# Softmax reciprocals sent through DRAM as rows instead of single numbers, and a later division

## The chip, the cores and the metric

One core of a Trainium2 chip runs the whole kernel. The metric is the device time of one execution in microseconds. The kernel before was timed three times: 1243.27, 1243.87 and 1244.43 us, a median of 1243.87. Every reading below is from one profiled execution, which took 1240.66 us with a span of 1238.9 us from its first to its last instruction.

## What is computed

The reference is two decoder layers on a sequence of 512 positions and a width of 1024. The change concerns the first layer's attention alone: 8 heads "A" (sparse attention: for each query only the 128 best keys of an index score count, with a bias by distance) and 8 heads "B" (forgetting attention: cumulated gates as bias), all causal. Cut to what matters:

```python
la = einsum('bthr,btkr->bhtk', ql, c_sel) + bias            # heads A
pa = softmax(where(valid, la, -inf));  oa = einsum('bhtk,btkr->bthr', pa, c_sel)
lb = einsum('bthd,bshd->bhts', qb, k_b) + fq - cum_f_keys   # heads B
pb = softmax(where(causal, lb, -inf)); ob = einsum('bhts,bshd->bthd', pb, v_b)
x  = layer_norm(ALPHA * x + concat([oa, ob]) @ w_o)
# then a convolutional FFN, and a second layer with gated mixers and another FFN
```

The softmax's division by the sum over keys may be done after the product with the values. The kernel does that.

## The kernel before

Every matrix product keeps float32 accuracy by three products: each operand is split into a rounded part and a rest ("hi" and "lo"), and `mm3` (lines 156 to 158) multiplies hi by hi, hi by lo and lo by hi. ScalarE makes hi by a cast, VectorE or GpSimd makes lo by a subtraction (`cut2`, lines 194 and 195, for results in PSUM).

Weights come as a stream of 192 units of 128 x 1024 numbers (`Stream`). SP issues the loads (line 60) into three raw buffers; `_split` casts on ScalarE (line 76) and subtracts on GpSimd (line 78) for the units of `POOL_CUT`, on VectorE (line 80) for the others. Unit 0 holds the index keys and gates, 1 to 4 the index queries, 5 the latent keys, 6 to 9 the values of heads B, 10 to 17 queries and keys of heads B in pairs, 18 to 22 those of heads A, 23 to 30 the output projection.

The 16 heads run in a software pipeline over `for h in range(18)`. The string `SEQ` gives the order within a turn: L the logits of head h (TensorE), B the bias of head h + 1 (GpSimd), T the transposes of head h - 1's probabilities (TensorE, then `cut2`), S the softmax of head h (VectorE adds the bias and takes the minimum of the negated logits, line 585; ScalarE takes exponentials and their sums, line 587), V the values of head h - 2 (TensorE). A digit takes so many steps of `fill`: projections of later heads' queries and keys, eight steps of three products a unit. `step` interleaves rounds of the choice of the best 128 keys on VectorE. The order within each engine's queue is settled at compile time by a list scheduler that starts from this order and may draw instructions forward; at run time each engine's queue works strictly in its order.

The product V yields the head's output transposed: 64 features on partitions, 512 positions along the row. The division needs the reciprocals of the sums along the row too, the same on all partitions, but `soft2` has them as 128 positions x 4 blocks. So they go through DRAM: `rd_d[h]` is written from `rd` with swapped axes (line 593), and `values` reads it back, broadcast to 64 partitions (line 626). Both are on SP's queue, as are the loads of weights. After every second head `values` multiplies (line 634), casts (635) and subtracts (636), the first and last of these on GpSimd for all pairs but the last.

Buffers: `tmp` holds eight tiles of 128 x 512 (the rows of gate sums `fks`, the choice's work tile, `t` and `rb` of `values`), `tri` is one group of three PSUM banks for the transposes, `psh` five banks for logits, values and fills, `dp` three tiles of probabilities `d`, `ptp` two of transposed ones. After the loop these PSUM pools are closed and eight banks opened for the output projection `out_ln`, whose first four units multiply heads B.

Of the kernel before, what the change touches and what calls it, by code (L numbers as in the profile page):

```python
# [9 lines left out]
F32 = mybir.dt.float32  # L10
FR = mybir.dt.float32r
AF = mybir.ActivationFunctionType
ALU = mybir.AluOpType
# [4 lines left out]
D = 1024  # L18
NCH = 4
# [6 lines left out]
EPS = 1e-5  # L26
BIG = 1e30
TAIL = 4
SEQ = "L2BT2SV2"
POOL_CUT = range(5, 23)  # L30
S1, S2, S3, S4 = 4, 3, 1, 2


def _f(ap):
    return ap.bitcast(F32)
# [59 lines left out]
def _body(ctx, tc, A):  # L95
    nc = tc.nc
# [6 lines left out]
    sm = E(tc.tile_pool(name="sm", bufs=4))  # L103
    dr = E(tc.tile_pool(name="dr", bufs=1, space=bass.MemoryType.DRAM))
# [4 lines left out]
    def bank():  # L109
        return ps[0].tile([128, 512], F32, name="bank")  # L110

    def temp():
        return tmp.tile([128, 512], F32, name="temp")

    def quad(dt=FR):
        return quads.tile([128, 4, 512], dt, name="quad")

    ws = Stream(nc, A["ws"], rawp, wp, 2)
    ws.on_pool = POOL_CUT
    base = [0]  # L120

    def unit():
        i = base[0]
        base[0] += 1
        return ws.get(i)
# [17 lines left out]
    ident = cst.tile([128, 128], F32)  # L143
# [10 lines left out]
    def mm3(out, a, b, first, last):  # L154

        nc.tensor.matmul(out, a[0], b[0], start=first, stop=False)  # L156
        nc.tensor.matmul(out, a[0], b[1], start=False, stop=False)  # L157
        return nc.tensor.matmul(out, a[1], b[0], start=False, stop=last)  # L158
# [12 lines left out]
    def proj(w, xt):  # L171
        p = bank()
        half(w, xt, p, 0, S)
        return p
# [8 lines left out]
    def proj_t(us, xt, n):  # L183

        p = bank()
        for k in range(8):
            o = (k % 2) * 512
            last_mm[0] = mm3(p, xk(xt, k, n * 128, n * 128 + 128), wk(us[k // 2], o, o + 512), k == 0, k == 7)
        return p

    def cut2(hi, lo, p, scale=1.0):

        if scale == 1.0:
            nc.scalar.copy(hi, p)
            dve[0] = nc.vector.tensor_tensor(out=lo, in0=p, in1=_f(hi), op=ALU.subtract)  # L195
        else:
            nc.scalar.mul(hi, p, scale)
            dve[0] = nc.vector.scalar_tensor_tensor(out=lo, in0=p, scalar=scale, in1=_f(hi),
                                           op0=ALU.mult, op1=ALU.subtract)
# [138 lines left out]
    with ExitStack() as m0:  # L338
# [9 lines left out]
        p = proj(w, xq)  # L348
# [7 lines left out]
        e = temp()  # L356
# [16 lines left out]
        for m in range(4):  # L373
            p = bank()
            half(unit(), xq, p, 128, S)
            for s, (a, b) in enumerate(((slice(0, 64), slice(64, 128)), (slice(64, 128), slice(0, 64)))):
                nc.scalar.mul(qi[s][a, m, lt], p[a, lt], float(HD ** -0.5))
                nc.vector.scalar_tensor_tensor(out=qi[s][b, m, lt], in0=p[a, lt], scalar=float(HD ** -0.5),
                                               in1=_f(qi[s][a, m, lt]), op0=ALU.mult, op1=ALU.subtract)

        p = bank()
# [9 lines left out]
        p = proj(unit(), xq)  # L391
# [5 lines left out]
        rb = mc.tile([32, NH], F32)  # L397
        nc.gpsimd.dma_start(rb, A["rel_bias"])
        p = bank()
        nc.tensor.matmul(p[:NH, :384], rb, oh[:32, :384], start=True, stop=True)  # L400
        t = temp()
# [3 lines left out]
        p = bank()  # L405
# [51 lines left out]
        def step(n=1):  # L457
            for _ in range(n):
                next(bg, None)
# [4 lines left out]
        for n in range(NCH):  # L464
            p = proj_t(us, xq, n)
# [83 lines left out]
        oq = []  # L549

        def dslice(d, j):
            return d[:, OFF[j]:OFF[j] + 128 * (j + 1)]

        st_ = {}
# [3 lines left out]
        def bias(h):  # L558
            if h < 16:
                biases[h] = (bias_b if h < 8 else bias_a)(h % 8)  # L560

        def logits(h):

            q = made[h // 2]
            d = biases.pop(h)
            r = slice(64 * (h % 2), 64 * (h % 2) + 64)
            b01, b2, b3 = bank(), bank(), bank()
            lg = [b01[:, :128], b01[:, 128:384], b2[:, :384], b3]
            for j in range(NCH):
                n = 128 * (j + 1)  # L570
                c = slice(j * 128, j * 128 + 128)
                mm3(lg[j], (q[r, 0, c], q[r, 1, c]), (q[r, 2, :n], q[r, 3, :n]), True, True)
            st_[h] = (d, lg)

        rd_d = dr.tile([16, NCH, 128], F32, name="rd_d")

        def soft(h):

            d, lg = st_[h]
            mn = sm.tile([128, 4], F32, name="mn")  # L580
            den = sm.tile([128, 4], F32, name="den")
            rd = sm.tile([128, 4], F32, name="rd")
            for j in range(NCH):
                dj = dslice(d, j)
                dve[0] = nc.vector.tensor_tensor_reduce(out=dj, in0=lg[j], in1=dj, scale=1.0, scalar=3e38,
                                               op0=ALU.add, op1=ALU.min, accum_out=mn[:, j:j + 1])
                nc.scalar.activation(dj, dj, AF.Exp, bias=mn[:, j:j + 1], scale=-1.0, accum_out=den[:, j:j + 1])
            st_[h] = (d, den, rd)

        def soft2(h):  # L590
            d, den, rd = st_[h]
            nc.vector.reciprocal(rd, den)
            nc.sync.dma_start(rd_d[h].rearrange("a b -> b a"), rd)

        PO = [0, 512, 896, 1152]

        def turn(h):
            d = st_[h][0]
            p = tri.tile([128, 1536], F32, name="tri")
            for i in range(NCH):  # L600
                for j in range(i, NCH):
                    o = PO[i] + (j - i) * 128
                    nc.tensor.transpose(p[:, o:o + 128], d[:, OFF[j] + i * 128:OFF[j] + i * 128 + 128], ident)
            pt = ptp.tile([128, 2, 1280], FR, name="pt")
            cut2(pt[:, 0], pt[:, 1], p[:, :1280])
            st_[h] = pt

        oq = []
        ot = {}

        def values(h):
            pt = st_.pop(h)
            if h % 4 == 0:
                oq.append(quad())
            i = h // 2
            o = (oq[-1][:, i % 2], oq[-1][:, 2 + i % 2])
            v = vB if h < 8 else vA
            b0 = 64 * (h % 2)
            r = slice(b0, b0 + 64)
            p = bank()  # L620
            m = b0 + 64
            hv = h % 8
            if h % 2 == 0:
                ot[i] = (temp(), temp())
            t, rb = ot[i]
            nc.sync.dma_start(rb[r], rd_d[h].rearrange("a b -> (a b)").partition_broadcast(64))
            for k in range(NCH):
                f = slice(64 * hv - b0, 64 * hv + 64)
                c = slice(PO[k], PO[k] + 512 - 128 * k)
                mm3(p[:m, k * 128:], (v[0][:, k, f], v[1][:, k, f]), (pt[:, 0, c], pt[:, 1, c]), k == 0, k == NCH - 1)  # L630
            nc.scalar.copy(t[r], p[r])  # L631
            if h % 2 == 1:
                eng = nc.gpsimd if h < 15 else nc.vector
                eng.tensor_tensor(out=t, in0=t, in1=rb, op=ALU.mult)
                nc.scalar.copy(o[0], t)
                eng.tensor_tensor(out=o[1], in0=t, in1=_f(o[0]), op=ALU.subtract)

        def work():
            for i in range(2, 4):
# [9 lines left out]
        def fill(n):  # L649
            for _ in range(n):  # L650
                next(todo, None)
# [2 lines left out]
        ps[0] = psum.enter_context(tc.tile_pool(name="psh", bufs=5, space=PSUM))  # L654
        tri = psum.enter_context(tc.tile_pool(name="tri", bufs=1, space=PSUM))
        bias(0)
        for h in range(18):
            for c in SEQ:
                if c == "L" and h < 16:
                    while h // 2 not in finished and next(todo, "end") != "end":  # L660
                        pass
                    logits(h)
                elif c == "B":
                    bias(h + 1)
                elif c == "S" and h < 16:
                    soft(h)
                    step(S3)
                    soft2(h)
                    step(S4)
                elif c == "T" and 1 <= h <= 16:  # L670
                    turn(h - 1)
                elif c == "V" and h >= 2:
                    values(h - 2)
                elif c.isdigit():
                    fill(int(c))
# [16 lines left out]
    with ExitStack() as m1:  # L692
# [17 lines left out]
        for n in range(NCH):  # L710
            p = proj_t(us, xt, n)
            if n < 2:
                late[n](last_mm[0])
            t = vp.tile([128, 8, HD], F32, name="vt")
# [12 lines left out]
            t = t.rearrange("p a b -> p (a b)")  # L727
# [5 lines left out]
        for n in range(NCH):  # L733
            p = proj_t(us, xt, n)
# [3 lines left out]
        for gp in range(4):  # L738
            p = bank()
# [5 lines left out]
            for j in range(2):  # L745
# [3 lines left out]
                    out=uq[:, :, f], in0=p[:, j * 256:j * 256 + 256].rearrange("p (a b) -> p a b", a=4),  # L749
                    scalar=sb[:, gi:gi + 1], in1=uq[:, :, f], op0=ALU.add, op1=ALU.mult)  # L750
        oq = [quad() for _ in range(4)]
        for ft in range(4):
            p = bank()
# [3 lines left out]
        for i in range(4):  # L757
# [5 lines left out]
            t = temp()  # L763
            nc.scalar.mul(t, y, ocw[:, i, 2:3])
            for dlt in (1, 2):
                nc.vector.scalar_tensor_tensor(out=t[:, dlt:], in0=y[:, :S - dlt], scalar=ocw[:, i, 2 - dlt:3 - dlt],
                                               in1=t[:, dlt:], op0=ALU.mult, op1=ALU.add)
            pb = proj(unit(), xt)
            nc.vector.tensor_tensor(out=t, in0=pb, in1=t, op=ALU.mult)
            q = oq[2 + i // 2]  # L770
# [95 lines left out]
```

## Time and profile before

| | |
|---|---|
| median of three runs | 1243.87 us |
| profiled execution | 1240.66 us |
| its span | 1238.9 us |
| TensorE busy | 1168.8 us, 94% of the span |
| VectorE busy | 685.8 us, 55% |
| ScalarE busy | 463.8 us, 37% |
| GpSimd busy | 201.9 us, 16% |
| mean granted TensorE clock | 0.971 |

Busy time on TensorE counts pipelined products whole, so neighbours overlap; the distance from start to start tells the rate. A slice is a fortieth of the span, 31 us; its digit is the busy share in tenths. A row of the waits reads: engine, line that waited, what released it, total us, times, longest. A row of the timeline reads: start, duration, engine, line, operation, output and inputs, count, and in brackets the idle time before it with its releaser. SPq is SP's queue of DMA issues; their duration is the issue alone, and landing is told apart.

### The profile page before, as it was taken

How to read it: one execution, taken by the hardware profiler on the slowest of the kernel's cores; microseconds unless marked ns; L12 is line 12 of the kernel's file. 1: busy time of each engine (PE TensorE's matmuls, PEld its weight loads, DVE VectorE, ACT ScalarE, POOL GpSimd, SP SyncE). 2: the span in 40 equal slices, each digit the busy share in tenths (PEclk: the TensorE clock that was granted, in tenths of full speed). 3: DMA queues.
4: the chain of work that ended last, by engine and by line, in shares of the span. 5: the costliest groups of instructions: out<-in, count | busy, mean ns of one | idle time of the engine just before them, and what ended most of it. 6: DMA issues, size and time to landing. Idle time of an engine off the chain costs nothing. (4 is left out here: it accounts for less than half of the span.)

```text
span 1238.9 us, 14423 instructions
## 1 busy us (share of the span) xinstructions
PE 1168.8 (94%) x5512; PEld 972.1 (78%) x5512; DVE 685.8 (55%) x1120; ACT 463.8 (37%) x693; POOL 201.9 (16%) x254
## 2 busy tenths in 40 slices
PE   7999998535999999999999999999999999999997
PEld 7787886434898888888888788888988888888886
DVE  6779854312656656656223885447565665662236
ACT  7525654422234443443222414233344344342121
POOL 3555653310300000000000420013000000000003
PEclk9999998767999999999999999999999999999999
DMA  6612511225213233234334313354123322344321
GB/s 227 216 66 69 94 14 30 60 61 179 93 60 98 90 102 102 88 106 147 121 118 170 111 52 121 126 184 166 60 94 102 102 88 99 102 140 149 102 85 69
DMA packets 49413, 132.03 MB, mean 107 GB/s; under 512 B 13800, under 2 KB 13808, under 8 KB 49344
## 3 DMA queue, kind: packets, MB, share of 16 engines
q1 hardware_dynamic: 44288, 115.39, 29.5%
q0 software_dynamic: 5056, 15.71, 4.1%
q8 instruction: 43, 0.70, 0.3%
q14 instruction: 26, 0.21, 0.1%
HBM read 122.63 MB, written 10.02 MB: 107 GB/s over the span
## 5 line engine op out<-in xcount | busy, mean ns | idle before, releaser
L156 PE MATMUL bank<-quad,whi 128*128 128x512 f32 (+2 forms) x932 | 356.5, 383 | 6.3 <-ACT quad L137 6.3
L157 PE MATMUL bank<-quad,whi 128*128 128x512 f32 (+2 forms) x932 | 355.6, 382 | 0.5 <-DVE quad L138 0.5
L158 PE MATMUL bank<-quad,wlo 128*128 128x512 f32 (+2 forms) x932 | 355.1, 381 | 0.0
L80 DVE TENSOR_TENSOR wlo<-raw,whi 128x1024 fp32r<-128x1024 f32 x150 | 183.6, 1224 | 291.3 <-ACT whi L76 290.6
L76 ACT CAST whi<-raw 128x1024 fp32r<-128x1024 f32 x161 | 169.6, 1053 | 262.0 <-PE bank L158 115.3
L156 PEld LDWEIGHTS bank<-quad,whi 128*128 128x128 f32 x932 | 176.1, 189 | 41.0 <-ACT quad L137 6.3
L157 PEld LDWEIGHTS bank<-quad,whi 128*128 128x128 f32 x932 | 176.5, 189 | 33.6 <-DVE quad L138 1.1
L158 PEld LDWEIGHTS bank<-quad,wlo 128*128 128x128 f32 x932 | 176.4, 189 | 32.9
L156 PE MATMUL bank<-whi,quad 128*128 128x512 f32 x388 | 151.5, 392 | 17.8 <-ACT temp L631 17.8
L157 PE MATMUL bank<-wlo,quad 128*128 128x512 f32 x388 | 151.6, 391 | 0.0
L158 PE MATMUL bank<-whi,quad 128*128 128x512 f32 x388 | 151.3, 390 | 0.0
L213 POOL DMA_DIRECT2D temp<-x x24 | 13.1, 548 | 567.9 <-ACT quadx L324 424.6
L156 PE MATMUL bank<-quad 128*128 128x512 f32 (+5 forms) x280 | 100.4, 362 | 2.3 <-DVE quad L195 1.4
L157 PE MATMUL bank<-quad 128*128 128x512 f32 (+5 forms) x280 | 98.7, 354 | 0.8 <-DVE quad L80 0.8
L156 PEld LDWEIGHTS bank<-whi,quad 128*128 128x128 f32 x388 | 73.2, 189 | 33.2 <-ACT temp L631 18.0
L158 PE MATMUL bank<-quad 128*128 128x512 f32 (+5 forms) x280 | 98.5, 353 | 0.0
L158 PEld LDWEIGHTS bank<-whi,quad 128*128 128x128 f32 x388 | 73.3, 189 | 15.3
L157 PEld LDWEIGHTS bank<-wlo,quad 128*128 128x128 f32 x388 | 73.3, 189 | 15.2
L293 DVE SCALAR_TENSOR_TENSOR temp<-bank,fcw,temp 128x511 f32<-128x511 f32 x88 | 65.4, 743 | 9.1 <-ACT temp L292 9.1
L80 DVE TENSOR_TENSOR quad<-raw,quad 128x1024 fp32r<-128x1024 f32 x24 | 31.2, 1306 | 68.3 <-ACT quad L76 67.9
L295 DVE SCALAR_TENSOR_TENSOR temp<-bank,fcw,temp 128x510 f32<-128x510 f32 x88 | 65.9, 748 | 3.0
L156 PEld LDWEIGHTS bank<-quad 128*128 128x128 f32 (+1 forms) x280 | 52.6, 189 | 14.6 <-issue 3.6
(148 smaller groups left out, 1293.0 us busy)
## 6 DMA issues: line engine op xcount, KB each, us to landing
raw<-in_ws_dram SPq DMA_DIRECT2D x192, 512.0 KB, 3.5
x<-temp SPq DMA_DIRECT2D x24, 256.0 KB, 2.0
temp<-x POOLq DMA_DIRECT2D x24, 256.0 KB, 3.2
temp<-in_xT_dram SPq DMA_DIRECT2D x8, 256.0 KB, 5.5
temp<-fk_d SPq DMA_DIRECT2D x8, 256.0 KB, 4.4
temp<-rd_d SPq DMA_DIRECT2D x16, 128.0 KB, 4.4
temp<-in_x_dram POOLq DMA_DIRECT2D x8, 256.0 KB, 8.3
quad<-in_ln_g_dram POOLq DMA_DIRECT2D x4, 512.0 KB, 6.0
```

Source lines behind the costliest of these rows:

```text
L76: nc.scalar.copy(hi, t)
L80: dve[0] = nc.vector.tensor_tensor(out=lo, in0=t, in1=_f(hi), op=ALU.subtract)
L156: nc.tensor.matmul(out, a[0], b[0], start=first, stop=False)
L157: nc.tensor.matmul(out, a[0], b[1], start=False, stop=False)
L158: return nc.tensor.matmul(out, a[1], b[0], start=False, stop=last)
L213: nc.gpsimd.dma_start(t, src[n * 128:n * 128 + 128, hf * 512:hf * 512 + 512])
L293: nc.vector.scalar_tensor_tensor(out=t[:, 1:], in0=p[:, :S - 1], scalar=cw[:, j, 1:2], in1=t[:, 1:], op0=ALU.mult, op1=ALU.add)
L295: nc.vector.scalar_tensor_tensor(out=t[:, 2:], in0=p[:, :S - 2], scalar=cw[:, j, 0:1], in1=t[:, 2:], op0=ALU.mult, op1=ALU.add)
```

## The change

The reciprocals of two heads (a pair) are gathered in one tile of 128 x 8. With the odd head's transposes TensorE turns them into 8 rows of 128; ScalarE copies the rows to SBUF and its own queue writes them to `rd_d`, whose layout is now 8 x 8 x 128. The read-back of both halves follows behind the pair's values, on SP. Multiplication, cast and subtraction move out of `values` into `divide`, which stands a head later, before the next V (the letter D), and the loop has two turns more for it. Pairs 0 to 3 divide on GpSimd, 4 to 7 on VectorE. `POOL_CUT` starts at unit 10 instead of 5: 13 units instead of 18 have their second part on GpSimd.

```diff
-SEQ = "L2BT2SV2"
-POOL_CUT = range(5, 23)
+SEQ = "L2BT2SDV2"
+POOL_CUT = range(10, 23)
...
-        rd_d = dr.tile([16, NCH, 128], F32, name="rd_d")
+        rd_d = dr.tile([8, 2 * NCH, 128], F32, name="rd_d")
+        rds = {}
...
         def soft2(h):
-            d, den, rd = st_[h]
-            nc.vector.reciprocal(rd, den)
-            nc.sync.dma_start(rd_d[h].rearrange("a b -> b a"), rd)
+            d, den = st_[h]
+            if h % 2 == 0:
+                rds[h // 2] = sm.tile([128, 8], F32, name="rd")
+            o = 4 * (h % 2)
+            nc.vector.reciprocal(rds[h // 2][:, o:o + 4], den)
...
+            if h % 2 == 1:
+                nc.tensor.transpose(p[:8, 1280:1408], rds.pop(h // 2), ident)
+                row = temp()[:8, :128]
+                nc.scalar.copy(row, p[:8, 1280:1408])
+                nc.scalar.dma_start(rd_d[h // 2], row)
             pt = ptp.tile([128, 2, 1280], FR, name="pt")
             cut2(pt[:, 0], pt[:, 1], p[:, :1280])
...
-                ot[i] = (temp(), temp())
-            t, rb = ot[i]
-            nc.sync.dma_start(rb[r], rd_d[h].rearrange("a b -> (a b)").partition_broadcast(64))
+                ot[i] = [temp()]
+            t = ot[i][0]
...
             if h % 2 == 1:
-                eng = nc.gpsimd if h < 15 else nc.vector
-                eng.tensor_tensor(out=t, in0=t, in1=rb, op=ALU.mult)
-                nc.scalar.copy(o[0], t)
-                eng.tensor_tensor(out=o[1], in0=t, in1=_f(o[0]), op=ALU.subtract)
+                rb = temp()
+                for e in range(2):
+                    nc.sync.dma_start(rb[64 * e:64 * e + 64], rd_d[i, 4 * e:4 * e + 4].rearrange(
+                        "a b -> (a b)").partition_broadcast(64))
+                ot[i].append(rb)
+
+        def divide(i):
+            t, rb = ot.pop(i)
+            q = oq[i // 2]
+            o = (q[:, i % 2], q[:, 2 + i % 2])
+            eng = nc.gpsimd if i < 4 else nc.vector
+            eng.tensor_tensor(out=t, in0=t, in1=rb, op=ALU.mult)
+            nc.scalar.copy(o[0], t)
+            eng.tensor_tensor(out=o[1], in0=t, in1=_f(o[0]), op=ALU.subtract)
...
-        for h in range(18):
+        for h in range(20):
...
+                elif c == "D" and h >= 4 and h % 2 == 0:
+                    divide(h // 2 - 2)
...
-                elif c == "V" and h >= 2:
+                elif c == "V" and 2 <= h <= 17:
                     values(h - 2)
```

More of the change, by code (lines that the diff above doesn't have):

```diff
@@ L581, in soft @@
             den = sm.tile([128, 4], F32, name="den")
-            rd = sm.tile([128, 4], F32, name="rd")
             for j in range(NCH):
@@ L587, in soft @@
                 nc.scalar.activation(dj, dj, AF.Exp, bias=mn[:, j:j + 1], scale=-1.0, accum_out=den[:, j:j + 1])
-            st_[h] = (d, den, rd)
+            st_[h] = (d, den)
         def soft2(h):
-            d, den, rd = st_[h]
-            nc.vector.reciprocal(rd, den)
-            nc.sync.dma_start(rd_d[h].rearrange("a b -> b a"), rd)
+            d, den = st_[h]
[3 more added lines that the diff above has]
+            nc.vector.reciprocal(rds[h // 2][:, o:o + 4], den)
         PO = [0, 512, 896, 1152]
@@ L615, in values @@
             i = h // 2
-            o = (oq[-1][:, i % 2], oq[-1][:, 2 + i % 2])
             v = vB if h < 8 else vA
```

## The prediction

> **What bounds the kernel now.** I read the 40 slices first, then the same stretch in windows, then who waited for whom in it, then SP's own waits and the transfers, then single instructions.
>
> ```profile
> PE   7999998535999999999999999999999999999997
> ```
> ```profile
> core 0: us, PE busy (x) PEld busy (x) DVE busy (x) ACT busy (x) POOL busy (x), PEclk, DMA share, GB/s
> 97.00:186.00 89.00, 89.00 (x479) 71.76 (x479) 69.77 (x183) 53.77 (x119) 51.37 (x78) 0.98 0.30 55
> 186.00:293.00 107.00, 56.73 (x285) 45.26 (x283) 30.27 (x70) 36.76 (x78) 27.03 (x38) 0.73 0.25 56
> ```
>
> TensorE has one hole, the seventh to the tenth slice. In the windows it lies between 186 and 293 us: 56.73 of 107 us busy, at a granted clock of 0.73, while no other engine is busy for even 37 us. Before it TensorE is full. So a wait holds this stage, not an engine's work. Next stand the waits of that window, SP's longest wait over the head loop, the transfers (KB each, us from issue to landing), the spread of the 16 reads' landings, and the ends of the chain on SP.
>
> ```profile
> POOL temp L634 <- DMA temp<-rd_d: 41.4, 3, 20.0
> ACT quad L635 <- POOL temp L634: 39.7, 4, 13.0
> ...
> PE bank L156 <- ACT pt L194: 26.0, 3, 14.4
> ...
> ACT quad L76 <- DMA raw<-in_ws_dram: 20.9, 1, 20.9
> ...
> PE bank L156 <- ACT temp L631: 17.8, 1, 17.8
> ```
> ```profile
> SPq L626 <- DMA rd_d<-rd: 156.8, 16, 11.7
> ```
> ```profile
> rd_d<-rd SPq DMA_DIRECT2D x16, 2.0 KB, 11.0
> ...
> tb_d<-temp POOLq DMA_DIRECT2D x1, 12.0 KB, 3.7
> ```
> ```profile
> DMA to landing us min/median/max: 2.7/4.4/12.5
> ```
> ```profile
> 101.73 0.38 SPq L593 DMA_DIRECT2D rd_d<-rd  x1
> ...
> 284.81 0.45 SPq L626 DMA_DIRECT2D temp<-rd_d  x1
> 285.32 33.94 SPq L60 DMA_DIRECT2D raw<-in_ws_dram  x10
> ```
>
> Read from the bottom up: SP issues write, read, write, read for 16 heads, one after the other. Each read waits until its own write of 2 KB has landed, 11.0 us after issue. From the first write to the last read are 183.1 us, 11.4 a head; 156.8 of them are this wait. The heads' own work needs less, so the chain falls ever further behind: the multiplication L634 waits for the read, ScalarE's cast L635 waits for L634, and as ScalarE works in order, the cast L194 of the next probabilities stands behind L635, and TensorE's value products stand behind L194 (26.0 us). The end of the stage is the same chain once more: SP's weight loads come behind the last read (285.32), ScalarE stands 20.9 us at a weight's cast L76, the copy L631 stands behind it, and TensorE waits 17.8 us for that copy, which frees the banks of the output projection.
>
> **How far the stage can shrink.** If nothing waits, TensorE's work remains. What is left of it from 165 to 292.8 us (rows grouped by shape), and the starts of single instructions at full clock:
>
> ```profile
> L603 PE MATMUL tri<-ident,d 128*128 128x128 f32 x90 | 14.0, 310 | 5.0 <-DVE pt L195 5.0
> ...
> L157 PE MATMUL bank<-quad,whi 128*128 128x512 f32 x27 | 11.3, 419 | 0.0
> ...
> L156 PE MATMUL bank<-pt,quad 128*128 128x512 f32 x6 | 3.5, 586 | 26.0 <-ACT pt L194 26.0
> L157 PE MATMUL bank<-quad 64*128 64x512 f32 x8 | 3.4, 422 | 0.0
> ...
> L156 PE MATMUL bank<-pt,quad 128*64 128x512 f32 x5 | 2.2, 437 | 0.0
> ```
> ```profile
> 182.44 0.39 PE L157 MATMUL bank<-quad,whi 128*128 128x512 f32 x1
> ...
> 184.05 0.39 PE L158 MATMUL bank<-quad,wlo 128*128 128x512 f32 x1
> 184.28 0.40 PE L156 MATMUL bank<-pt,quad 128*128 128x512 f32 x1
> ...
> 186.12 0.45 PE L156 MATMUL bank<-quad,whi 128*128 128x512 f32 x1
> ...
> 187.66 0.33 PE L156 MATMUL bank<-quad 64*128 64x128 f32 x1
> ...
> 189.77 0.50 PE L156 MATMUL bank<-quad,whi 128*128 128x512 f32 x1
> ...
> 191.27 1.25 PE L603 MATMUL tri<-ident,d 128*128 128x128 f32 x10
> 192.28 0.48 PE L156 MATMUL bank<-quad,whi 128*128 128x512 f32 x1
> ...
> 223.64 0.51 PE L156 MATMUL bank<-pt,quad 128*128 128x512 f32 x1 [2.80 <-ACT pt L194]
> 225.16 2.39 PE L603 MATMUL tri<-ident,d 128*128 128x128 f32 x10 [1.02 <-DVE pt L195]
> ...
> 292.85 0.80 PE L156 MATMUL bank<-whi,quad 128*128 128x512 f32 x1 [17.80 <-ACT temp L631]
> ```
>
> Busy times overlap, so I take start to start. A 512-wide product takes 0.23 us (182.44 to 184.05 is seven), one head's values 1.84 (184.28 to 186.12), its logits 2.11 (187.66 to 189.77), its ten transposes 1.01 (191.27 to 192.28). Left are 27 x 3 fill products (18.6), 11 heads of values (6 + 5 rows; 20.2), 8 of logits (16.9), 9 of transposes (9.1): 64.8 us. From 165.2 us, where the next product starts, TensorE could be done at 230.0. The first product of the output projection starts at 292.85 now; 62.8 us is the most that this edit can free there.
>
> **The change part by part.**
>
> Writes. The 16 strided writes of 128 x 4 single numbers become 8 writes of 8 rows of 512 bytes, on ScalarE's queue. No row has this shape; the nearest is tb_d, 8 rows to DRAM, 3.7 us from GpSimd's queue. I take 3.7; ends: 2.7, the fastest of the reads, and 11.0, as now. SP keeps 16 reads at 4.4 us, in pairs, each pair behind one write: even one after the other, 8 x (3.7 + 4.4) = 65 us against 183, shorter than the 133 us that TensorE needs from 97 on, so the chain no longer paces the heads. SP's loads of weights wait behind a read for about 3.7 us, and the 20.9 us at the end go.
>
> TensorE. Eight more transposes (128 x 8 into 8 x 128), five of them after 165 us: a tenth of 1.01 each, +0.5 us (nothing to 2: a product of its own at 0.4 each). The reciprocals stay on VectorE.
>
> ScalarE. Each pair adds a row copy and one issue ahead of the odd head's cast L194. The nearest copy, 8 x 384 from PSUM, took 0.474; for a third of its columns I take 0.25, and 0.45 for an issue as SP's read shows. Six pairs lie beside fills, which cover it; for the last two it is on the path: +1.4 (ends 0 and 5.6, all eight).
>
> ```profile
> L402 ACT ACTIVATE temp<-bank 8x384 f32<-8x384 f32 x1 | 0.5, 474 | 0.0
> ```
>
> The last heads. From head 12 on no fill is left. Two heads that ran without the chain start their exponentials 5.48 us apart; TensorE's part of a head is 4.96. Four heads: +2.1. Then the pipeline drains: one bank group for transposes, so head 15's transposes wait for head 14's cast and subtraction (1.22 + 1.49), and its own values for its own: about 4 us more idle TensorE (ends 2 and 7).
>
> ```profile
> 225.35 0.40 ACT L587 ACTIVATE d<-d,mn 128x128 f32<-128x128 f32 x1
> ...
> 230.83 0.40 ACT L587 ACTIVATE d<-d,mn 128x128 f32<-128x128 f32 x1 [0.75 <-DVE mn L585]
> ```
> ```profile
> L195 DVE TENSOR_TENSOR pt<-tri,pt 128x1280 fp32r<-128x1280 f32 x16 | 23.8, 1486 | 14.8 <-ACT pt L194 14.8
> L194 ACT CAST pt<-tri 128x1280 fp32r<-128x1280 f32 x16 | 19.6, 1223 | 5.2 <-PE tri L603 5.0
> ```
>
> The clock. After 2.80 us of waiting at 223.64 the ten transposes took 2.39 instead of 1.25: some 2 us lost. I take one such loss in the drain, +2. The Trainium skill, "TensorE: Matmul & The Clock Gate", section "What's actually happening", lets the clock halve only after an idle window of about 3.4 us; by that the term would be 0 for gaps as short as mine, and the forecast 2 us lower. The row with 2.80 us speaks against it, so I keep 2.
>
> The division. It moves a head later, in front of the values on its engine. The last four pairs go to VectorE: 8 x 0.684 = 5.5 us more there, beside 30.3 in the window above, well under its room; GpSimd loses three pairs, on no path. But a multiplication that comes early stands at VectorE's head, and behind it the next head's minimum and subtraction wait. From the transposes, copy, write and read need 0.25 + 0.45 + 3.7 + 4.4 = 8.8 us; a division two heads on comes 11.0 after them, one that is ordered up to the pair's values about 7. I take 3 us in all for four pairs (ends 0 and 20).
>
> ```profile
> L634 DVE TENSOR_TENSOR temp<-temp 128x512 f32<-128x512 f32 x1 | 0.7, 684 | 0.0
> ```
>
> Five units (5 to 9) go from GpSimd to VectorE: 5 x 1.306 = 6.5 us more there, most of it between 30 and 40 us. VectorE is busy 2.92 of 10 us there and GpSimd 9.98, which is relieved; TensorE is full, so nothing is to be gained: 0, and +6.5 should VectorE's idle time not cover it.
>
> ```profile
> L80 DVE TENSOR_TENSOR quad<-raw,quad 128x1024 fp32r<-128x1024 f32 x24 | 31.2, 1306 | 68.3 <-ACT quad L76 67.9
> ```
> ```profile
> 30.00:40.00 10.00, 10.00 (x52) 8.06 (x51) 2.92 (x6) 6.20 (x10) 9.98 (x6) 1.00 0.65 191
> ```
>
> **The sum.** 230.0 + 0.5 + 1.4 + 2.1 + 4 + 2 + 3 = 243.0 us for the first product of the output projection, 49.9 earlier. The first products there run slow now (0.80 at 292.85 against 0.39 warm); starting warm returns about 1 us. Total -50.9. The profiled execution took 1240.66 us (1.76 outside its span), 3.2 below the median of 1243.87: 1189.8 on its scale, 1193 on the median's.
>
> **The rivals.**
>
> *A new wait in place of the old (22%).* The new write stays as slow as the old (11.0), or write and read land late behind weights. Then a pair has its reciprocals 0.7 + 11.0 + 4.4 = 16.1 us after the transposes against 11.0: VectorE stands 5 us for each of four pairs, 20 instead of 3: 1210. For it: reads landed up to 12.5 us after issue, and the weight loads that SP could not send before 285 now run in the same stretch. Against: the one write to DRAM in rows landed in 3.7. The Trainium skill, "DMA: Bandwidth & Descriptors", section "Issuing engines are not separate DMA queues", says that ScalarE's transfers run on the same engines as SP's and only save issue time; no run here yet shows ScalarE's queue.
>
> *The other side (5%).* ScalarE's queue takes over SP's wait: if each write must wait for the previous pair's write and read (11.0 + 4.4 = 15.4 us, the ends above) while ScalarE holds everything behind it, 8 x 15.4 = 123 plus its own work from 97 to 293 (53.8 + 36.8 = 90.5) is 213.7, so the projection starts near 311, 18 later: 1262. It decides from (196 - 90.5)/8 = 13.2 us a pair. Against: all 16 long waits on SP stand at the reads, none at a write, though each write there follows a read of the same tensor.
>
> *No gain (3%).* The heads' own chain, not the transfer, makes the hole: 1244. Against it the 5.48 us between heads that did not wait.
>
> **How the numbers follow.** My forecast holds 70%. Its own range: with the low ends (0.5 + 2.1 + 2 beside 230.0, so 8.4 us less) 1185, with the high ends of copies, drain and units (4.2 + 3 + 6.5 more) 1207. The new wait, with the same ends added in part, reaches to 1216, and 1180 lets the clock and the early stage give a little more: 1180 to 1216 leaves out some 15%. The bound between faster and same is 0.2%, 2.5 us, about what these runs can tell. Faster 0.92, same 0.03, slower 0.05.
>
> **What would show it.** Right: SP's 156.8 us at L626 shrink below 50; the write lands in under 5 us; TensorE is above 85% between 186 and 240 at a clock above 0.9; the projection's first product starts near 243; the first 165 us stay. Wrong: waits of VectorE or ScalarE for the read above 10 us, or a start after 255.

## The result, and the profile after

The changed kernel takes 1193.11 us (median of four, 1190.69 to 1194.73) against 1243.57 for the kernel before beside it: a ratio of 0.960, interval 0.957 to 0.963. Forecast were 1193 and faster. The profiled execution took 1192.23 us with a span of 1190.2.

The slices of TensorE and then the windows, columns as before:

```profile
PE   7999999889999999999999999999999999999997
```
```profile
97.00:165.00 68.00, 68.00 (x364) 54.58 (x363) 58.28 (x156) 41.72 (x96) 37.68 (x59) 0.97 0.21 69
...
186.00:240.00 54.00, 48.92 (x288) 38.97 (x286) 33.85 (x76) 37.09 (x80) 19.23 (x32) 0.98 0.30 89
```

The hole is closed: from 186 to 240 us TensorE is busy for 48.92 of 54 us at a granted clock of 0.98, and by then all heads are done. Up to 165 us nothing moved. Below stand the landings of the reads, SP's wait at them, the last pair's row copy, cast and write on ScalarE, and on SP the last pair of reads with the loads behind it.

```profile
DMA to landing us min/median/max: 2.9/3.0/5.0
```
```profile
SPq L640 <- DMA rd_d<-temp: 69.1, 8, 23.5
```
```profile
233.62 0.25 ACT L609 COPY temp<-tri 8x128 f32<-8x128 f32 x1
233.79 1.21 ACT L194 CAST pt<-tri 128x1280 fp32r<-128x1280 f32 x1
233.91 0.30 ACTq L610 DMA_DIRECT2D rd_d<-temp  x1
```
```profile
236.46 1.08 SPq L640 DMA_DIRECT2D temp<-rd_d  x2
237.64 27.76 SPq L60 DMA_DIRECT2D raw<-in_ws_dram  x8
```

The landing of the writes on ScalarE's queue is not recorded, but the read that waits for the last one is issued 2.55 us after it (233.91 to 236.46), where a write of single numbers took 11.0. SP's 69.1 us at the reads cost little: a read now stands at the head of SP's queue before its pair's second head is even computed, for 23.5 us at the longest, and no wait for the read-back is left on VectorE, GpSimd or ScalarE. Only loads of weights still stand behind these reads, and that counts at the end of the stage.

The end of the stage, TensorE first, then ScalarE:

```profile
230.31 1.31 PE L605 MATMUL tri<-ident,d 128*128 128x128 f32 x10 [0.99 <-DVE pt L195]
...
235.05 0.50 PE L156 MATMUL bank<-pt,quad 128*128 128x512 f32 x1 [1.81 <-ACT pt L194]
236.57 0.50 PE L157 MATMUL bank<-pt,quad 128*128 128x512 f32 x1 [1.02 <-DVE pt L195]
...
238.28 0.41 PE L157 MATMUL bank<-pt,quad 128*128 128x128 f32 x1
...
244.33 0.80 PE L156 MATMUL bank<-whi,quad 128*128 128x512 f32 x1 [5.42 <-ACT temp L636]
```
```profile
231.61 1.99 ACT L76 CAST quad<-raw 128x1024 fp32r<-128x1024 f32 x2
...
238.22 1.04 ACT L76 CAST quad<-raw 128x1024 fp32r<-128x1024 f32 x1 [2.75 <-DMA raw<-in_ws_dram]
242.63 1.04 ACT L76 CAST quad<-raw 128x1024 fp32r<-128x1024 f32 x1 [3.37 <-DMA raw<-in_ws_dram]
243.70 0.58 ACT L636 COPY temp<-bank 64x512 f32<-64x512 f32 x1
```

The output projection starts at 244.33 us instead of 292.85, 48.5 us earlier, and the span is 48.7 shorter. So all of the gain lies before this point. One wait of the old kind is left: TensorE stands 5.42 us because the copy L636, which frees the banks, stands in ScalarE's queue behind two casts of weights that wait for their loads. SP still has a part in it. VectorE's subtraction L80, which frees the raw buffer for the second of these loads, ended at 235.05 us, but the load was issued at 237.64, behind the last pair's two reads, and its cast started at 242.63.

This makes a simple measure for all that follows: start of the projection's first product, and the rest from there to the end of the span.

| kernel | start, us | span - start, us |
|---|---|---|
| before | 292.85 | 946.05 |
| changed | 244.33 | 945.87 |

### The profile page after: what moved, and what is told of

It is laid out like the page before. It is cut to its first block, busy times and chain, and to the rows that moved or that the text cites. A ratio compares the mean times of both kernels' runs of the same rounds, so it can differ in the third digit from the quotient of the medians.

```text
span 1190.2 us, 14421 instructions
## 1 busy us (share of the span) xinstructions
PE 1160.6 (98%) x5520; PEld 967.1 (81%) x5520; DVE 691.2 (58%) x1131; ACT 465.6 (39%) x701; POOL 186.2 (16%) x243
## 5 line engine op out<-in xcount | busy, mean ns | idle before, releaser
L80 DVE TENSOR_TENSOR wlo<-raw,whi 128x1024 fp32r<-128x1024 f32 x151 | 185.0, 1225 | 292.4 <-ACT whi L76 291.7
L156 PEld LDWEIGHTS bank<-whi,quad 128*128 128x128 f32 x388 | 73.3, 189 | 20.9 <-ACT temp L636 5.6
L292 ACT ACTIVATE temp<-bank,fcw 128x512 f32<-128x512 f32 x88 | 59.9, 681 | 10.8 <-PE bank L158 10.8
```

What stands on the lines that cost most here:

```text
L80: dve[0] = nc.vector.tensor_tensor(out=lo, in0=t, in1=_f(hi), op=ALU.subtract)
L292: nc.scalar.mul(t, p, cw[:, j, 2:3])
```

## The experiments

The theory: the landing time of the strided write, 16 times in a row on SP, made the chain, and its shortening is the gain. Rivals: the later division (ScalarE no longer holds the next cast), the queue that issues the write, and the five units. The first four runs share one chip (kernel before: 1238.73 us), the next four another (1252.44). Ratios are therefore compared within a group.

**Five units back to GpSimd.**

```diff
-POOL_CUT = range(10, 23)
+POOL_CUT = range(5, 23)
```

> The changed kernel with units 5 to 9 given back to GpSimd (18 units there, as before). My theory: the five subtractions lie beside other work on either engine, so 1193, within 2 us of the changed kernel's 1193.1. Rival: they are on the path of the first 60 us and cost or give up to 5 x 1.3 = 6.5 us: 1187 or 1200.

Measured: 1184.65 us, ratio 0.956 (0.954 to 0.958). That is lower than "within 2 us" allowed, toward the rival. ScalarE and TensorE at the end of the stage:

```profile
236.30 1.04 ACT L76 CAST quad<-raw 128x1024 fp32r<-128x1024 f32 x1 [2.83 <-DMA raw<-in_ws_dram]
237.37 0.58 ACT L636 COPY temp<-bank 64x512 f32<-64x512 f32 x1
```
```profile
238.00 0.50 PE L156 MATMUL bank<-whi,quad 128*128 128x512 f32 x1 [1.53 <-ACT temp L636]
```

Only one waiting cast stands ahead of the copy here, and TensorE waits 1.53 us instead of 5.42. So either the units or this order, which the scheduler chose anew, makes the difference; the last group tells which.

**Rows alone.** The changed kernel with the division right behind its pair's values on GpSimd (but for the last pair), and 18 units there:

```diff
-SEQ = "L2BT2SDV2"
+SEQ = "L2BT2SV2"
...
                 ot[i].append(rb)
+                divide(i)
...
-            eng = nc.gpsimd if i < 4 else nc.vector
+            eng = nc.gpsimd if i < 7 else nc.vector
```

> Only the way of the reciprocals is new: transposed, written as rows by ScalarE's queue. The division follows its pair's values at once, on GpSimd for seven pairs, and 18 units are on GpSimd, all three as before. My theory: the write's landing time made the chain, so nearly all of the gain is here; the division may wait about 2 us a pair for the read, and some of that is hidden: 1193 to 1201, and SP's waits at the reads well under 100 us in all. Rival theory (the later division is what frees ScalarE): most of the gain is gone, 1225 or more.

Measured: 1185.83 us, ratio 0.957 (0.955 to 0.958). What waits for the read-back, and the start of the projection:

```profile
DVE temp L650 <- DMA temp<-rd_d: 2.5, 1, 2.5
```
```profile
240.62 0.50 PE L156 MATMUL bank<-whi,quad 128*128 128x512 f32 x1 [0.67 <-ACT temp L636]
```

The whole gain is here, without the later division. The early division waits once, 2.5 us, at the last pair, beside the projection. The time lies below the 1193 to 1201 us that I had written: TensorE waits only 0.67 us for the last copy here, not 5.42, and the rest of the span from there on is 943.6 us, not 945.87.

**The later division alone**, on the kernel before, writes of single numbers on SP:

```diff
-SEQ = "L2BT2SV2"
+SEQ = "L2BT2SDV2"
...
-            if h % 2 == 1:
-                eng = nc.gpsimd if h < 15 else nc.vector
-                eng.tensor_tensor(out=t, in0=t, in1=rb, op=ALU.mult)
...
+        def divide(i):
...
+                elif c == "D" and h >= 4 and h % 2 == 0:
+                    divide(h // 2 - 2)
```

> Only the division is later (a head later, pairs 0 to 3 on GpSimd, 4 to 7 on VectorE). The reciprocals are still written as single numbers by SP's queue, each read behind its write. My theory: SP's chain stays at 11 us a head, its waits stay near 150 us, the last read stays near 285 us, and a division that is one head later waits all the same: 1232 to 1246. Rival theory (who waits counts, not the chain's length): ScalarE no longer holds the casts, 1195 to 1210.

Measured: 1236.15 us against 1238.73, ratio 0.997 (0.995 to 0.999). SP's waits, the waits for the read-back, and TensorE:

```profile
SPq L625 <- DMA rd_d<-rd: 150.3, 16, 12.2
```
```profile
DVE temp L637 <- DMA temp<-rd_d: 13.2, 1, 13.2
POOL temp L637 <- DMA temp<-rd_d: 12.0, 2, 10.6
```
```profile
262.44 0.80 PE L156 MATMUL bank<-pt,quad 128*128 128x512 f32 x1 [14.89 <-ACT pt L194]
...
283.10 0.79 PE L156 MATMUL bank<-whi,quad 128*128 128x512 f32 x1 [15.71 <-ACT temp L630]
```

As the theory has it: the chain is nearly as long as ever, so a wait that is put off by a head is met all the same, now on VectorE too. It runs from 101.1 to 275.4 us, 174.3 us against 183.1, because the write landed in 10.1 us (median) on this occasion; I had expected the last read near 285. The rival is out.

**Single numbers on ScalarE's queue**, no transposes, the rest as changed:

```diff
             nc.vector.reciprocal(rds[h // 2][:, o:o + 4], den)
+            nc.scalar.dma_start(rd_d[h // 2, o:o + 4].rearrange("a b -> b a"), rds[h // 2][:, o:o + 4])
...
-                nc.scalar.dma_start(rd_d[h // 2], row)
```

> The changed kernel, but the reciprocals are written as 512 single numbers a head again, now by ScalarE's queue, with no transposes and no row copies. My theory (the write's landing time counts through the chain of write and read on one queue): the writes land 11 us after issue but no longer wait for each other's reads; a pair is read back 16 us after its second head's reciprocals, 5 us after the division could start, so VectorE waits about 5 us at each of the last four pairs: about 1208 (1199 to 1218). Rival (it is only the queue: one queue's order made the chain): 1193 to 1196. Other rival (single numbers keep the transfer engines so busy that the weights come late): 1225 or more.

Measured: 1200.55 us, ratio 0.968 (0.966 to 0.971), against 0.956 and 0.957 for the two kernels with rows beside it. The landings of the reads and the writes, a wait for the read-back, and TensorE:

```profile
temp<-rd_d SPq DMA_DIRECT2D x16, 128.0 KB, 5.7
...
rd_d<-rd ACTq DMA_DIRECT2D x16, 2.0 KB, 10.8
```
```profile
DVE temp L645 <- DMA temp<-rd_d: 6.2, 1, 6.2
```
```profile
228.21 0.79 PE L156 MATMUL bank<-pt,quad 128*128 128x512 f32 x1 [6.05 <-ACT pt L194]
...
249.28 0.80 PE L156 MATMUL bank<-whi,quad 128*128 128x512 f32 x1 [4.34 <-ACT temp L632]
```

The time is in the range I had written, at its low end, and both halves of the gain show. A landing of 10.8 us hurts much less once the writes no longer stand in line with their reads: about three quarters of the gain are there (1 - 0.968 of 1 - 0.957), and the later division, which this kernel also has, brought only 0.3% alone. The last quarter is not all the write's landing. 3 to 4 us of it are the wait for the last copy (4.34 us here, 1.53 and 0.67 in the two kernels beside it). And where I had written 5 us at each of four pairs, VectorE stood 6.2 us at one, for a read that was itself late: the reads landed 5.7 us after issue in the median and 17.4 at the longest, with rows 3.0 and 5.0. Why they land late beside single numbers is not shown.

**The end of the stage, and the queue.** Four kernels beside each other on another chip. First the changed kernel again:

> The changed kernel again, beside the next three on one chip. Expected 0.960 of the kernel before.

Measured: 1190.58 us, ratio 0.951 (0.949 to 0.953). The kernel before took 1252.44 here, 9 us more than in the first comparison, so all ratios of this group lie below those I had written, and the differences between its kernels are what counts. The changed kernel's projection starts so:

```profile
242.89 0.79 PE L156 MATMUL bank<-whi,quad 128*128 128x512 f32 x1 [5.65 <-ACT temp L636]
```

Then the changed kernel with one ordering rule, which puts the casts of units 27 to 30 behind the last copy (`c` is the cast in `_split`):

```diff
-            nc.scalar.copy(t[r], p[r])
+            last_copy[0] = nc.scalar.copy(t[r], p[r])
...
+        def behind(i, c):
+            if 27 <= i <= 30:
+                tc.add_manual_dep(c.ins, last_copy[0].ins.name, AFTER, reason="...")
+
+        ws.behind = behind
```

> The changed kernel with one ordering rule: ScalarE's casts of weight units 27 to 30 come behind the last copy L636, which frees the banks for the output projection. In the changed kernel two of these casts stood ahead of that copy, waiting 2.75 and 3.37 us for their loads, and TensorE waited 5.42 us. My theory: those two waits are what is left at the stage's end, the copy comes at 239.4 instead of 243.7 us and the kernel is 4.3 us faster than the changed one (0.9565 of before); what giving five units back to GpSimd won was this order, not the units. Rival: the units' later casts stop TensorE inside the projection, and the time is given back, within 1 us of the changed kernel. Second rival: the units themselves cost 4 us in the first 60 us, then it stays above the kernel with units given back.

Measured: 1180.77 us, ratio 0.943 (0.941 to 0.945), 9.8 us below the changed kernel beside it.

```profile
234.15 0.58 ACT L640 COPY temp<-bank 64x512 f32<-64x512 f32 x1 [2.77 <-PE bank L161]
234.76 2.00 ACT L77 CAST quad<-raw 128x1024 fp32r<-128x1024 f32 x2
```
```profile
234.79 0.50 PE L159 MATMUL bank<-whi,quad 128*128 128x512 f32 x1 [0.67 <-ACT temp L640]
```

And the same rule with 18 units on GpSimd:

> The same ordering rule on the kernel with 18 units on GpSimd. In that kernel one waiting cast (2.83 us) stood ahead of the last copy and TensorE waited 1.53 us. My theory: 1 us faster than with units back alone, and the same as the previous kernel within 1.5 us, as the units lie beside other work: 0.955 to 0.9565 of before. Rival (the units cost 4 us of their own): 0.953 or less, clearly below the previous kernel.

Measured: 1181.14 us, ratio 0.943 (0.941 to 0.946).

```profile
236.35 0.51 PE L159 MATMUL bank<-whi,quad 128*128 128x512 f32 x1 [0.67 <-ACT temp L640]
```

With the order set alike, 13 and 18 units on GpSimd are the same within their intervals. The units lie beside other work, as forecast; what the first experiment won was the place of one copy in a queue. (This kernel is 3.5 us below the one of the first experiment, on the other chip, where I had expected 1.) The kernel with the rule on 13 units is 9.8 us faster where I expected 4.3. Four parts add up to it: the wait before the projection is 0.67 instead of 5.65 (5.0); the last head's values no longer wait 1.6 us for a cast L194 behind two casts of weights; the projection starts warm, so that the rest of the span is 944.11 instead of 945.81 (1.7); and 1.4 lies between 97 and 101 us, where both kernels run the same products in the same order, but at a granted clock of 0.50 (98 to 100 us) in the one profile and 1.00 in the other. That part is not the rule's. This is the fastest version, 0.943 of the kernel before.

Last, the row writes on SP, with TensorE's, VectorE's and GpSimd's orders unchanged:

```diff
-                nc.scalar.dma_start(rd_d[h // 2], row)
+                nc.sync.dma_start(rd_d[h // 2], row)
```

> The changed kernel, its row writes issued by SP instead of ScalarE; TensorE's, VectorE's and GpSimd's orders stay the same. My theory: rows land in under 3 us on either queue, a pair's chain on SP is 3 + 3 us against over 11 us of a pair's work, and ScalarE saves eight issues: within 2 us of the changed kernel, 0.958 to 0.962. Rival (the queue counts): write, read, write, read on SP make a chain again, weights come late: 0.975 or more.

Measured: 1189.22 us, ratio 0.950 (0.948 to 0.951), the changed kernel's within the intervals.

```profile
SPq L610 <- ACT temp L609: 65.9, 8, 21.9
...
SPq L640 <- DMA rd_d<-temp: 8.3, 8, 2.1
```
```profile
242.22 0.79 PE L156 MATMUL bank<-whi,quad 128*128 128x512 f32 x1 [6.54 <-ACT temp L636]
```

SP now waits for the row copy; write and read stand in turn on one queue again, but SP's waits for the write's landing are 8.3 us in all, 2.1 at the longest, and the projection starts no later than in the changed kernel. So it is not ScalarE's queue that makes rows fast. The Trainium skill, "DMA: Bandwidth & Descriptors", section "Issuing engines are not separate DMA queues", says that another issuing engine only saves issue time; for rows these two runs agree. With single numbers the other queue won much, but by taking the writes out of SP's order: their landing was 10.8 us there too.

**The kernel before once more**, as its median had been 1243.6, 1238.7 and 1252.4 us while the changed kernel's hardly moved.

> The kernel before once more, for its profile on another occasion: its median was 1243.6, 1238.7 and 1252.4 us in three comparisons, the changed kernel's only 1193.1 and 1190.6. My theory: the chain of 16 writes of single numbers sets its time, so the time follows the landing: span minus 1238.9 equals the change of the chain's length from first write to last read (183.1 us), within 2 us. Rival: the difference lies elsewhere (the clock in the stages that are full), and the chain is within 2 us of 183.1 whatever the span.

Measured: one execution, 1254.9 us, span 1253.1 (one more beside it took 1253.26). The landing, SP's waits, the ends of the chain, and the start of the projection:

```profile
rd_d<-rd SPq DMA_DIRECT2D x16, 2.0 KB, 11.8
```
```profile
SPq L626 <- DMA rd_d<-rd: 165.6, 16, 12.4
```
```profile
102.76 0.38 SPq L593 DMA_DIRECT2D rd_d<-rd  x1
...
298.39 0.45 SPq L626 DMA_DIRECT2D temp<-rd_d  x1
```
```profile
306.30 0.80 PE L156 MATMUL bank<-whi,quad 128*128 128x512 f32 x1 [19.43 <-ACT temp L631]
```

The chain is 195.6 us long instead of 183.1: 12.5 more, with the span 14.2 longer, of which 1.0 lies before the chain. The rest from the projection on is 946.8 us against 946.05, so the rival is out. With the later division alone as a third profile the figures line up: landings of 10.1, 11.0 and 11.8 us, chains of 174.3, 183.1 and 195.6, starts of the projection at 283.10, 292.85 and 306.30. The landing of the strided write differs by occasion, and the kernel before takes it over 16 times. The ratio of 0.951 to 0.960 for one and the same change fits this; the runs of 1252.44 us left no profile to show it.

Starts and rests of all, the rest being the span less the start:

| kernel | start, us | span, us | rest, us |
|---|---|---|---|
| units back | 238.00 | 1181.9 | 943.9 |
| rows alone | 240.62 | 1184.2 | 943.6 |
| later division alone | 283.10 | 1230.5 | 947.4 |
| single numbers on ScalarE's queue | 249.28 | 1195.2 | 945.9 |
| changed, again | 242.89 | 1188.7 | 945.8 |
| copy first | 234.79 | 1178.9 | 944.1 |
| copy first, units back | 236.35 | 1179.9 | 943.6 |
| rows on SP | 242.22 | 1187.7 | 945.5 |
| before, once more | 306.30 | 1253.1 | 946.8 |

## Why the prediction was right

The mechanism was the one forecast, and the sum came out at 243.0 us against a start of 244.33. But that it came out so well is luck. TensorE's own work was put about 4 us too low and a wait of 4.8 was missing, while other terms were about 7 us too dear: 3 for the division, 2.1 for the last heads, about 1.5 for the clock, the rest for copies and drain.

- *The chain.* Right, and shown: with the division as before, rows alone bring it all; with the chain as before, the later division brings 0.3%; and when the landing grew by itself the chain and the span grew together.
- *TensorE's work, up to 230.0 us.* Too low. From 165.16 us, where the prediction's first product starts, to the end of the last value product at 238.90 TensorE is idle for 4.0 us and at work for 69.7, not 64.8 + 0.5. I had priced every 512-wide product at 0.23 us; behind another kind of work the first one takes longer (0.31 from 182.18 to 182.49, behind transposes). The clock cost under 1 us of it; whether such first products make up all of the rest is not shown.
- *The last heads, 2.1, and five more transposes, 0.5.* The transposes cost what was taken: with the eleventh the group takes 1.12 us (191.31 to 192.43) instead of 1.01. The other term's wait is not there: before the first gap of the drain (0.99, at 230.31) TensorE is idle for 0.17 us in all.
- *The write, 3.7 us.* At most 2.55 here. *The read, 4.4:* 3.0. Both were somewhat too dear.
- *SP's waits below 50 us.* Wrong: 69.1. I took a wait of SP for a cost; SP waits because its reads stand early in its queue. Only the last of these waits is seen to cost something.
- *Row copy and issue, 1.4.* The copy took 0.25 as taken, but the issue (0.30 at 233.91) runs beside the cast that began at 233.79: at most 0.5 for the last two pairs.
- *The wait of the division, 3.* It is not there. It stands in the kernel with single numbers, where one pair cost 6.2.
- *The drain, 4, and the clock, 2.* The gaps are 0.99, 1.81 and 1.02, so 3.8, but the middle one is not the wait I forecast: two casts of weights (231.61, 1.99 us) stood ahead of the row copy and the cast L194. With the copy first this gap is not there and the drain is 2.0, so the size came out by luck. The clock cost less than 1 us before the last product (0.41 at 238.28 where such a product takes 0.28). The row with 2.80 us, by which I kept the 2, was also misread: the next row that the prediction shows has a wait of 1.02, so TensorE stood idle for 3.8 of the 4.3 us before the slow transposes.
- *"The 20.9 us at the end go."* This step failed. Of the weight casts' wait ahead of the last copy, 2.75 + 3.37 were left, and TensorE stood 5.42. I counted some 3.7 us for which a load stands behind a read (the second of these stood 2.6, from 235.05 to 237.64), but put no term for it into the sum, and did not ask who stands behind a cast whose load is still under way. Had the copy been first, the wait would have been 0.67 as in the kernel with the rule, so this is 4.8 us that the sum lacked; without it the start would have been about 239.6, 3.4 earlier than forecast.
- *Starting warm, 1 us back.* It did not come (0.80 at 244.33, rest 945.87 against 946.05), because of that same wait. With the copy first it came: 1.7.
- *The units, 0.* Right by the pair of kernels with the copy first. But a change that costs nothing by itself moved the scheduler's order, and that was worth several us.

Of the rivals, the new wait is what single numbers on ScalarE's queue show, though its reads were late too: about 15 us beside the two kernels with rows in that comparison and 7 to 10 beside the changed kernel in the others, where I had put 17 on it. Nothing was seen of ScalarE holding a pair's write and read, nor of a hole made by the heads alone.

## What to carry to other kernels

Here a small transfer was paid by its landing, not by its size (2 KB of single numbers 11.0 us, 4 KB of rows at most 2.55), and most dearly where write and read took turns on one in-order queue: count the turns and multiply. Shortening it, or letting the writes go without waiting for the reads, was worth far more than using the result later. When a stage's main wait goes, look at once at what stands in each in-order queue behind the next load that is still under way; here one copy behind two casts held 5 us, and a small ordering rule won them back.

## What was not expected of the hardware

- The landing of 512 single numbers to DRAM was 11.0 us (median) in one profile of the same kernel and 11.8 in another; the chain of 16 was 12.5 us longer with it, and the span 14.2.
- The reads of 128 KB, the same in all kernels, landed in 2.9 to 3.3 us (median, 5.3 at most) in the kernels with rows and in 4.4 to 5.7 (17.4 at most) in those with single numbers. No run here shows why.
- An issue on ScalarE's queue (0.30 us) ran beside ScalarE's cast, not between two instructions.
- The clock fell after two waits of 1.81 and 1.02 us, before the long wait (granted clock 0.90 from 237 to 238 us, then 0.50). The Trainium skill, "TensorE: Matmul & The Clock Gate", section "What's actually happening", gives an idle window of about 3.4 us for it; no single wait was that long, but with other work between them they lie within 3.4 us of each other (233.2 to 236.6). In the changed kernel's second profile (1.62 and 1.02) and with the units back (2.09 and 1.03) the clock did not fall before the last value product, so the length of such waits alone does not settle it.
